# SiLU as one ScalarE function in the state space branch, and its norm one output unit later

## The chip, the cores and the metric

The kernel runs on one core of a Trainium2 chip. The metric is the device time of one execution in microseconds. TensorE (PE) multiplies matrices into PSUM banks, VectorE (DVE) does elementwise work, ScalarE (ACT) evaluates a function of scale times input plus bias, GpSimd (POOL) does a little elementwise work here, and the queue of SyncE (SP) issues the DMAs. Each engine works through its own instructions in order, and semaphores join the engines.

## The reference, cut to what matters

Two layers on a residual stream x of 512 tokens and 1024 channels. Each layer projects x into three branches, a state space branch (SSD), differential attention and cross-attention to 256 memory tokens; the branches are gated, summed, projected and normalised. The SSD branch is what the change touches:

```
xbc = silu(centred_dwconv(xbc, conv_w) + conv_b)         # 5 taps per channel, 3072 channels
xs, B, C = split(xbc)                                    # 2048, 4 x 128, 4 x 128 channels
dt = softplus(dt_raw + dt_bias); a = -exp(a_log)
y  = ssd_scan(xs*dt, dt*a, B, C) + the same backwards + d_skip*xs
y  = y * silu(z)
y_ssd = y * rsqrt(mean(y*y) + 1e-5) * norm_w             # mean over all 2048 channels
```

with silu(v) = v / (1 + exp(-v)) = v/2 * (1 + tanh(v/2)).

## The kernel before

Channels lie on the 128 partitions and the 512 tokens in the free dimension. All large products run in fp32r with each factor split in two (`split`: a rounded copy on ACT, the remainder on DVE) and three matmuls per pair. Weights come in units of 128x1024 values: one DMA into `wr` (2 buffers), the split into `wh` and `wl` (3 buffers each), then 24 matmuls of 512 columns into a bank `pj` (3 banks). `emit` walks a list of jobs (`self.T`), and asks for the weights of the next two units ahead of each job. The order of the jobs in the list is their priority; a planner at build time orders the instructions of every engine by priority and by when its own costs say that operands and buffers are there. `self.late` shifts priorities (`LX` for the transposes of xs, `LD` for the last product of a head pair).

The SSD branch of a layer runs over four groups g. A group has one unit for B, one for C, four for xs, then the chunk states, and then for b = 0 to 3 a unit for z (`zpart`) and the scan's output `ypart(g, b)` for two heads. Ready units of the next group fill PE while a `ypart` waits. From group 1 on the output units of the group before (`wpart(g-1, u)`) are listed behind the xs units; those of the last group stand at the end.

`conv` (from L432) brings one unit through convolution and SiLU. With `hcw`, half of the weights and bias, ACT writes `acc` from the PSUM bank with the centre tap, DVE adds four taps (`acc<-pj,hcw,acc`), ACT takes `th` = tanh(acc), and DVE forms (th + 1) * acc, which is the SiLU of twice `acc`. The result goes to `bC`, `cC` or `xsC` and from there to PE. `zpart` does the same on z, but without the half: `sz` = (tanh(z/2) + 1) * z is twice the SiLU, y is twice its value, and the epsilon of the norm is four times the reference's to make up for it.

`ypart` has per head a DMA that spreads a row of decays over all partitions (`ab<-dab`, 2 buffers), a mask on DVE (`ab<-ab,cst`), 8 `Exp` activations (`ab<-ab,bias`), and two DVE operations to `m`, which PE multiplies with `xsT` (`pm<-m,xsT`). Then DVE combines y, and ACT and DVE split it into `yh` and `yl`; ACT squares it into the buffer of `sz` (2 buffers), and POOL adds the square to `sqa`. `dt_tables`, once a layer in group 0, prepares the decays with `Exp`, `Ln` and `Exp` again.

`norm` multiplies the four blocks of `sqa` with ones on PE, takes a reciprocal root by 12 small DVE operations behind the mean, spreads it by matmuls with the identity, and ACT copies it to `rB`. `fin(j)` multiplies the gate and `rB` into the output rows. The end of the branch is listed as: gate units 0 and 1, `norm`, gate unit 2, `wpart(3, 0..3)`, and then gate units 3 to 7 with `fin(0..7)`. The gates take the tags `th` and `sz` with two buffers each.

Of the kernel before, what the change touches and what calls it, by code (L numbers as in the profile page):

```python
# [14 lines left out]
AF = mybir.ActivationFunctionType  # L15
ALU = mybir.AluOpType
# [4 lines left out]
P = 128  # L21
S = 512
# [4 lines left out]
EPS = 1e-5  # L27
# [6 lines left out]
PCW, PCB, PNW, PGB, PDN, PLG, PLB, PDS, NP_ = 0, 120, 144, 160, 184, 185, 193, 201, 217  # L34
# [17 lines left out]
def bc(ap, shape):  # L52
    return ap.broadcast_to(shape)


class Net:
# [243 lines left out]
    def layer_params(self, l):  # L300
        nc, a = self.nc, self.a
        pr = self.t(self.cp, [P, NP_], "pr", bufs=2)
        nc.sync.dma_start(out=pr, in_=a["pk"][l])
        self.par = pr
        self.hgb = self.t(self.cp, [P, 24], "hgb", bufs=2)
        self.ts(self.hgb, pr[:, PGB:PGB + 24], 0.5, ALU.mult)
        self.hcw = self.t(self.cp, [P, 144], "hcw", bufs=2)
        self.ts(self.hcw, pr[:, PCW:PCW + 144], 0.5, ALU.mult)


    def mem_kv(self, l):
# [121 lines left out]
    def conv(self, ps, ci, out):  # L433

        sp = self.sp
        acc = self.t(sp, [P, S], "acc", bufs=2)
        th = self.t(sp, [P, S], "th", bufs=2)
        cw = lambda j: self.hcw[:, ci * 5 + j:ci * 5 + j + 1]
        self.act(acc, ps, AF.Identity, scale=cw(2), bias=self.hcw[:, 120 + ci:121 + ci])
        for j in (-2, -1, 1, 2):  # L440
            o, i = slice(max(0, -j), S - max(0, j)), slice(max(0, j), S - max(0, -j))
            self.stt(acc[:, o], ps[:, i], cw(2 + j), acc[:, o], ALU.mult, ALU.add)
        self.act(th, acc, AF.Tanh)
        self.stt(out, th, 1.0, acc, ALU.add, ALU.mult)

    def ssd(self, l):
        nc = self.nc
# [75 lines left out]
        def zpart(g, b):  # L523
            def f(wh, wl):
                ps = self.proj(wh, wl)
                th = self.t(self.sp, [P, S], "th", bufs=2)
                self.act(th, ps, AF.Tanh, scale=0.5)
                self.sz = self.t(self.sp, [P, S], "sz", bufs=2)
                self.stt(self.sz, th, 1.0, ps, ALU.add, ALU.mult)
            return f  # L530

        def ypart(g, b):
# [56 lines left out]
        def wpart(g, u):  # L589
            def f(wh, wl):  # L590
                yh, yl = self.yhl[g]
                for i in range(2):
                    ps = self.bank(self.pj, "pj")
                    for k in range(4):
                        c = slice(k * 256 + i * P, k * 256 + (i + 1) * P)
                        self.mm3(ps, wh[:, c], wl[:, c], yh[:, k, :], yl[:, k, :], k == 0, k == 3)
                    o = self.br[:, 2 * u + i, :]
                    if g == 0:
                        self.act(o, ps)
                    else:  # L600
                        self.tt(o, o, ps, ALU.add)
            return f
# [6 lines left out]
        def norm():  # L609
            sp = self.sp  # L610

            pt = self.bank(self.pt, "pt")
            for c in range(4):
                self.mm(pt[:, c:c + 1], self.sqa[:, c * P:(c + 1) * P], self.ones[:, 0:1])
            ms = self.t(sp, [P, 4], "ms")
            self.ts(ms, pt[:, 0:4], 1.0 / 2048.0, ALU.mult, 4.0 * EPS, ALU.add)
            r = self.rsqrt(sp, ms, 4)
            pr = self.bank(self.pm, "pm")
            for c in range(4):
                self.mm(pr[:, c * P:(c + 1) * P], bc(r[:, c:c + 1], [P, P]), self.ident)  # L620
            self.rB = self.t(sp, [P, S], "acc", bufs=2)
            self.act(self.rB, pr)

        def gpart(j):
            def f(wh, wl):
                self.gt[j] = self.gate(self.sp, wh, wl, 0, j, "th" if j % 4 < 2 else "sz")
            return f

        def fin(j):
            def f():  # L630
                t, o = self.gt.pop(j), self.br[:, j, :]
                self.stt(t, t, 1.0, self.rB, ALU.add, ALU.mult)
                self.tt(o, o, t, ALU.mult)
            return f
# [29 lines left out]
        self.gt = {}  # L664
        for j in range(3):
            self.T(gpart(j), (l, UGL + j))
            if j == 1:
                self.T(norm)
        for u in range(4):
            self.T(wpart(3, u), (l, UBS + 12 + u))  # L670
        for j in range(KC):
            if j + 3 < KC:
                self.T(gpart(j + 3), (l, UGL + j + 3))
            self.T(fin(j))
# [638 lines left out]
```

## Time and profile before

| | |
|---|---|
| time, median of 3 runs | 2211.78 us (2208.17 to 2215.52) |
| the profiled execution | 2208.37 us, of which the span of the instructions is 2206.5 us |
| granted TensorE clock, mean | 0.995 |
| PE, DVE, ACT busy | 2158.8, 1609.6, 1022.9 us |
| the SSD branch in the trace, layer 0 and layer 1 | about 20 to 460 us, and 1150 to 1615 us |
| ACT table loads | 7, 9.0 us |

The profile shows one execution. Busy shares of PE are not its distance from full speed: matmuls overlap. What PE could still gain is read from what it waits for. "A <- B: us, times" in a list of waits says that A stood idle until B ended. In a row of the chain or of a time line the first number is the start in microseconds from the first instruction, the second the duration; the time in square brackets is the engine's idle time before it. Names are written as output<-inputs, and L103 is line 103.

### The profile page before, as it was taken

To read this page: it belongs to the slowest core of one execution; us is meant where nothing else is said; L and a number is where in the kernel's file an instruction comes from. 1 tells how busy PE (TensorE), PEld (TensorE's weight loads), DVE (VectorE), ACT (ScalarE), POOL (GpSimd) and SP (SyncE) were. 2 spreads that over 40 slices of the span, in tenths; PEclk is the share of its full clock that TensorE was granted. 3 is DMA by queue.
4 is the path that set the end of the run, shared out by engine and by line. 5 is a ranking of instruction groups with operands and counts; after the bars stand their busy time and mean duration, and the time that the engine had idled before them with its cause. 6 is when DMAs were issued, how large, how long until landed. Compare 5 with 4: busy or idle time off the path is not lost.

```text
span 2206.5 us, 29202 instructions
## 1 busy us (share of the span) xinstructions
PE 2158.8 (98%) x11122; PEld 1780.2 (81%) x11122; DVE 1609.6 (73%) x2486; ACT 1022.9 (46%) x1935; POOL 52.7 (2%) x38
## 2 busy tenths in 40 slices
PE   8999999999999999999999999999999999999998
PEld 6777877778888888887887777777788888888876
DVE  7897888858554778866467887888754547788667
ACT  5664546424432555543345564555423325555430
POOL 0000000000000000000000000000100000000000
PEclk9999999999999999999999999999999999999999
DMA  4654544335553433324564654444434334333253
GB/s 151 172 171 129 157 133 147 111 95 174 164 170 120 134 110 111 108 88 153 157 220 111 169 143 143 143 141 137 120 99 130 111 109 136 111 110 106 90 159 109
DMA packets 109680, 295.27 MB, mean 134 GB/s; under 512 B 12460, under 2 KB 13028, under 8 KB 109284
## 3 DMA queue, kind: packets, MB, share of 16 engines
q1 hardware_dynamic: 109540, 293.41, 44.1%
q8 instruction: 87, 1.43, 0.3%
q14 instruction: 53, 0.43, 0.1%
HBM read 255.06 MB, written 17.33 MB: 123 GB/s over the span
## 4 chain that ended last, share of the span: by engine, by line
PE 76%; DVE 11%; DMA 7%; ACT 3%; issue 2%; POOL 0%; SPq 0%; POOLq 0%; DVEq 0%; ACTq 0%
PE pj L103 59%; PE pm L103 15%; DMA ab<-dab 5%; PE pt L111 2%; DVE ab L81 2%; DVE wl L81 2%; DVE acc L84 2%; DVE y L81 1%; DMA wr<-wu 1%; ACT wh L91 1%; ACT ab L91 1%; DVE yl L84 1%; DVE m L81 1%; DMA fth<-rd 1%; DVE eb L81 1%
## 5 line engine op out<-in xcount | busy, mean ns | idle before, releaser
L103 PE MATMUL pj<-xh,wl 128*128 128x512 f32 x1664 | 663.8, 399 | 5.5 <-ACT mrg L91 3.8
L103 PE MATMUL pj<-xh,wh 128*128 128x512 f32 x1664 | 659.5, 397 | 6.9 <-ACT xh L91 6.0
L103 PE MATMUL pj<-xl,wh 128*128 128x512 f32 x1664 | 658.7, 396 | 0.0
L81 DVE TENSOR_TENSOR wl<-wr,wh 128x1024 fp32r<-128x1024 f32 x330 | 404.8, 1227 | 102.4 <-ACT wh L91 101.9
L91 ACT ACTIVATE wh<-wr 128x1024 fp32r<-128x1024 f32 x330 | 347.3, 1053 | 215.8 <-PE pj L103 139.5
L103 PEld LDWEIGHTS pj<-xh,wh 128*128 128x128 f32 x1664 | 313.5, 188 | 79.1 <-ACT xh L91 6.0
L103 PEld LDWEIGHTS pj<-xh,wl 128*128 128x128 f32 x1664 | 313.6, 188 | 76.5 <-ACT mrg L91 5.5
L103 PEld LDWEIGHTS pj<-xl,wh 128*128 128x128 f32 x1664 | 313.8, 189 | 66.2 <-issue 4.2
L91 ACT ACTIVATE ab<-ab,bias 128x128 f32<-128x128 f32 x512 | 160.7, 391 | 117.9 <-DVE ab L81 116.1
L84 DVE SCALAR_TENSOR_TENSOR acc<-pj,hcw,acc 128x510 f32<-128x510 f32 (+1 forms) x192 | 141.6, 742 | 26.5 <-ACT acc L91 25.5
L941 DVE TENSOR_REDUCE fmx<-pm 128x1 f32<-128x512 f32 x128 | 85.0, 685 | 47.0 <-PE pm L103 47.0
L103 PE MATMUL pj<-yl,wh 128*128 128x512 f32 x256 | 103.8, 406 | 0.8 <-DVE yl L84 0.8
L103 PE MATMUL pj<-yh,wh 128*128 128x512 f32 x256 | 104.4, 408 | 0.0
L103 PE MATMUL pj<-dy,wh 128*128 128x512 f32 (+1 forms) x384 | 102.6, 356 | 1.3 <-DVE dy L81 1.3
L81 DVE TENSOR_TENSOR ab<-ab,cst 128x1024 f32<-128x1024 f32 x64 | 85.7, 1338 | 24.1 <-DMA ab<-dab 24.0
L103 PE MATMUL pj<-yh,wl 128*128 128x512 f32 x256 | 103.2, 404 | 0.1
L91 ACT ACTIVATE fpp<-pm,fmx 128x512 f32<-128x512 f32 x128 | 87.2, 686 | 33.6 <-DVE fmx L941 33.6
L103 PE MATMUL pj<-cy,wh 128*128 128x512 f32 x256 | 78.8, 389 | 0.0
L103 PEld LDWEIGHTS pj<-dy,wh 128*128 128x128 f32 x384 | 67.5, 188 | 13.7 <-DVE dy L81 2.6
L103 PE MATMUL pj<-wh,xl 128*128 128x256 f32 x256 | 73.3, 286 | 0.0
L103 PE MATMUL pj<-wl,xh 128*128 128x256 f32 x256 | 72.4, 283 | 0.0
L103 PE MATMUL pj<-wh,xh 128*128 128x256 f32 x256 | 72.4, 283 | 0.0
(280 smaller groups left out, 3317.2 us busy)
## 6 DMA issues: line engine op xcount, KB each, us to landing
wr<-wu SPq DMA_DIRECT2D x336, 512.0 KB, 3.7
ab<-dab SPq DMA_DIRECT2D x64, 512.0 KB, 5.6
eb<-deb SPq DMA_DIRECT2D x64, 256.0 KB, 4.8
mkv<-dkv SPq DMA_DIRECT2D x16, 512.0 KB, 3.9
rsw<-rx SPq DMA_DIRECT2D x64, 128.0 KB, 2.3
dy<-dy SPq DMA_DIRECT2D x32, 256.0 KB, 2.3
dgt<-tg SPq DMA_DIRECT2D x16, 256.0 KB, 4.2
dkv<-mo SPq DMA_DIRECT2D x16, 256.0 KB, 4.3
```

What stands on the lines that cost most here:

```text
L81: (eng or self.nc.vector).tensor_tensor(out=out, in0=a, in1=b, op=op)
L84: self.nc.vector.scalar_tensor_tensor(out=out, in0=a, scalar=s, in1=b, op0=op0, op1=op1)
L91: self.nc.scalar.activation(out=out, in_=a, func=f, **kw)
L103: self.nc.tensor.matmul(out=out, lhsT=a, rhs=b, start=first, stop=last)
L111: self.nc.tensor.transpose(out=out, in_=x, identity=self.ident)
L941: nc.vector.tensor_reduce(out=mx[:, c:c + 1], in_=ps, axis=AX.X, op=ALU.min)
```

## The change

In `conv` the full weights and bias are used in place of their halves, `hcw` is gone, and ACT's own SiLU function writes the result from `acc`; the tile `th` and the DVE operation behind it are gone. In `zpart` ACT's SiLU writes `sz` straight from the PSUM bank; again `th` and one DVE operation are gone. As y is no longer doubled, the norm's epsilon is the reference's. `norm` moves in the list from behind gate unit 1 to behind `wpart(3, 0)`, past gate unit 2 and that output unit.

```
@@ layer_params
-        self.hcw = self.t(self.cp, [P, 144], "hcw", bufs=2)
-        self.ts(self.hcw, pr[:, PCW:PCW + 144], 0.5, ALU.mult)
@@ conv
-        th = self.t(sp, [P, S], "th", bufs=2)
-        cw = lambda j: self.hcw[:, ci * 5 + j:ci * 5 + j + 1]
-        self.act(acc, ps, AF.Identity, scale=cw(2), bias=self.hcw[:, 120 + ci:121 + ci])
+        cw = lambda j: self.par[:, PCW + ci * 5 + j:PCW + ci * 5 + j + 1]
+        self.act(acc, ps, AF.Identity, scale=cw(2), bias=self.par[:, PCB + ci:PCB + ci + 1])
...
-        self.act(th, acc, AF.Tanh)
-        self.stt(out, th, 1.0, acc, ALU.add, ALU.mult)
+        self.act(out, acc, AF.Silu)
@@ zpart
-                th = self.t(self.sp, [P, S], "th", bufs=2)
-                self.act(th, ps, AF.Tanh, scale=0.5)
                 self.sz = self.t(self.sp, [P, S], "sz", bufs=2)
-                self.stt(self.sz, th, 1.0, ps, ALU.add, ALU.mult)
+                self.act(self.sz, ps, AF.Silu)
@@ norm
-            self.ts(ms, pt[:, 0:4], 1.0 / 2048.0, ALU.mult, 4.0 * EPS, ALU.add)
+            self.ts(ms, pt[:, 0:4], 1.0 / 2048.0, ALU.mult, EPS, ALU.add)
@@ the list of the branch's end
         for j in range(3):
             self.T(gpart(j), (l, UGL + j))
-            if j == 1:
-                self.T(norm)
         for u in range(4):
             self.T(wpart(3, u), (l, UBS + 12 + u))
+            if u == 0:
+                self.T(norm)
```

## The prediction

> **What bounds the kernel now.** I read the page's busy times and its chain first, then the list of what PE waits for, then the busy times in the two stretches in which the state space branch (SSD) runs.
>
> ```profile
> PE 2158.8 (98%) x11122; PEld 1780.2 (81%) x11122; DVE 1609.6 (73%) x2486; ACT 1022.9 (46%) x1935; POOL 52.7 (2%) x38
> ...
> PE 76%; DVE 11%; DMA 7%; ACT 3%; issue 2%; POOL 0%; SPq 0%; POOLq 0%; DVEq 0%; ACTq 0%
> ```
>
> PE carries 76% of the chain and is hardly ever idle. Work taken from DVE, or put on ACT, counts only where PE stops for it. PE's waits over the whole span say how much there is to win; these are the rows whose tiles belong to the SSD branch (us in total, times, longest).
>
> ```profile
> PE pm L103 <- DVE m L81: 8.3, 8, 2.2
> ...
> PE pt L103 <- POOL sqa L81: 4.4, 2, 2.4
> PE pm L103 <- DVE xw L81: 4.4, 2, 2.6
> PE pj L103 <- ACT mrg L91: 3.8, 4, 2.3
> ...
> PE pt L111 <- DVE bC L84: 1.0, 2, 0.7
> ...
> PE pm L103 <- DVE cC L84: 0.8, 2, 0.5
> ```
>
> Together they are 22.7 us, 1.0% of the time. The change takes nothing from PE itself, so this is about the ceiling of a gain; a loss has no such ceiling. The room on the other engines is in the table of stretches (length, then PE, PEld, DVE, ACT, POOL busy us; layer 0, then layer 1):
>
> ```profile
> 60.00:455.00 395.00, 385.30 (x1943) 303.51 (x1942) 332.54 (x456) 211.59 (x450) 26.46 (x16) 1.00 0.49 145
> 1190.00:1607.00 417.00, 403.05 (x2017) 317.90 (x2016) 343.63 (x475) 217.06 (x458) 24.98 (x16) 0.99 0.50 141
> ```
>
> DVE is at 84% and 82%, ACT at 54% and 52%. So the change takes load from the fuller of the two.
>
> **The SiLU: what goes.** Groups by line and shape, of ACT and of DVE:
>
> ```profile
> L91 ACT ACTIVATE th<-acc 128x512 f32<-128x512 f32 x48 | 30.2, 629 | 39.3 <-DVE acc L84 39.3
> ...
> L91 ACT ACT_TABLE_LOAD x7 | 9.0, 1283 | 0.8 <-PEq L1304 0.7
> ```
> ```profile
> L84 DVE SCALAR_TENSOR_TENSOR xsC<-th,acc 128x512 f32<-128x512 f32 x32 | 22.0, 687 | 4.0 <-ACT th L91 4.0
> L84 DVE SCALAR_TENSOR_TENSOR sz<-th,pj 128x512 f32<-128x512 f32 x32 | 21.9, 685 | 27.5 <-ACT th L91 23.6 <-POOL sqa L81 3.6
> ```
>
> The 48 convolutions and the 32 z units each lose one DVE operation, 80 x 0.686 = 54.9 us of DVE. The profile has no SiLU activation. The nearest row is the tanh of the same shape, 629 ns, and I take the same: ACT's pure work stays. The scaling of the convolution's weights once a layer, at the layer's head, I cost at nothing either way; PE is then busy with the products before it.
>
> What does it win on the path? The waits for `bC` and `cC` (1.0 + 0.8) are each shorter than the 0.69 us that leave their chain, so they go: **-1.8 us** (from 0 to -1.8). For the 8 waits on `m` I looked into the chain of waits, in group 0 of both layers:
>
> ```profile
> 99.15 0.60 DVE sz L84
> 99.75 0.61 DVE ab L81
> ...
> 100.38 0.70 DVE m L81
> ```
> ```profile
> 1239.98 0.60 DVE sz L84
> ...
> 1252.39 0.60 DVE sz L84
> ```
>
> Three times the removed operation stands in DVE's queue right ahead of the sum and the product that make `m`. 3 x 0.60 gives **-1.8 us**. The bounds are 0, if DVE's queue only closes up behind the mask's DMA, and -8.3, if all of these waits go.
>
> **The SiLU: what comes.** Seven table loads in the whole kernel show that tanh and `Exp` share a table (they alternate without one), and that other functions do not share it. Around `Ln` in `dt_tables`:
>
> ```profile
> 52.64 1.28 ACT L91 ACT_TABLE_LOAD   x1
> 54.91 0.42 ACT L91 ACTIVATE bias<-bias 128x256 f32<-128x256 f32 x1 [0.99 <-DVE bias L88]
> ```
> ```profile
> 58.12 0.28 ACT L91 ACTIVATE cum<-pm 128x128 f32<-128x128 f32 x1 [1.00 <-PE pm L103]
> 58.42 1.28 ACT L91 ACT_TABLE_LOAD   x1
> 59.71 0.63 ACT L91 ACTIVATE th<-acc 128x512 f32<-128x512 f32 x1
> 60.25 0.26 ACT L91 ACTIVATE dtot<-pm 128x128 f32<-128x128 f32 x1
> 60.41 1.06 ACT L91 ACTIVATE eb<-pt 64x512 f32<-64x512 f32 x2
> ```
>
> Whether SiLU stands in `Exp`'s table no row can say; the nearest rows, of `Ln` and back, say no, and I take that. Counting in ACT's order every change between a future SiLU (`th<-acc`, and `th` of z) and an `Exp` (`dtot`, `wst`, `ab<-ab,bias`), as from the row at 59.71 to the row at 60.25, I get 102 changes. That is 102 x 1.283 = 131 us more on ACT, 65 us in each stretch, which brings it to 70% and 68%. The bounds of the number of loads are 0 and, if the planner mixes more, about 160 (two for each of 80 SiLUs).
>
> How much of a load delays anybody? The first pair of rows shows the mechanism: the load runs at once, while the function behind it still waits for its operand, and costs nothing. The second shows the other case: ACT is late, and `th` starts 1.31 us after `cum` ends. `Exp` mostly waits:
>
> ```profile
> ACT ab L91 <- DVE ab L81: 116.1, 37, 5.5
> ```
>
> 37 waits of 3.1 us on average cover 37 of the 51 loads ahead of an `Exp`; 14 of 51, 27%, stay open. Ahead of a convolution's SiLU the wait is 39.3 us in all (row of `th<-acc`), 0.8 for each of 48; I count half of these loads as open. So about (14 + 25) x 1.28 = 50 us of lateness lies on ACT in stretches where it has 383 us idle. Weights do not suffer: in PE's waits above, ACT appears for `mrg` alone.
>
> On the path this gives three terms. (1) `dt_tables`, once a layer: in the rows above `dtot` and `eb` (an `Exp` each) come right behind a `th` with no pause, and the rows that PE waits for (`xw`, twice) hang on them. One more load each: **+2.6 us** (from 0 to two loads each, +5.1). (2) The 8 waits on `m` lengthen by the open 27% of a load: 8 x 0.27 x 1.28 = **+2.8 us**. (3) The four waits on `mrg`, by the mean open share 39 of 102: 4 x 0.38 x 1.28 = **+2.0 us**. The bounds of (2) and (3) are 0 and what the rivals below make of them.
>
> One wait changes engine. The DVE row of `sz` has waited 3.6 us for POOL, which still reads the old square out of the buffer. Now ACT writes `sz` itself and would stand there, with the next weight split and the next head's `Exp`s queued behind it. I put it at zero, as the planner holds the SiLU back until it sees the buffer free.
>
> The Trainium skill (ScalarE: Activation LUTs, section What ACT_TABLE_LOAD costs) speaks against this change: it counts a drain of about 1380 ns beside the 1283 ns, 2.66 us for each change of set. By that the 102 changes would be an estimated 271 us. The trace disagrees: from the end of `cum` at 58.40 to the start of `th` at 59.71 there is room for the load and nothing else.
>
> **The norm.** In the chain at the end of layer 0's branch (a unit of 24 matmuls is the measure):
>
> ```profile
> 422.64 5.49 PE pj L103 x24
> ...
> 449.25 1.27 POOL sqa L81
> ...
> 450.56 1.05 PE pt L103 x8
> ```
>
> PE stands until POOL has added the last square. Moved past a gate unit and an output unit, the sums come up to 11 us later in PE's list, while POOL is 2.4 us late at most: the wait goes, **-4.4 us** for both layers (0, if the planner had already placed the output unit ahead). What moves: 8 matmuls on `sqa`, 13 small DVE operations, 8 spreading matmuls, one ACT copy; no DMA. Behind it stand the `fin`s, which need `rB`; three further output units, 3 x 5.49 = 16.5 us, cover that. What would be late next is `wpart(3, 0)` itself, which needs the last `yl`; it needs it only for the last quarter of its first bank, 9 matmuls in, 9 x 5.49/24 = 2.1 us, and the gate unit ahead of it gives 5.5 us more. If that cover is gone, the part of POOL's lateness that DVE shares returns, at most the 4.4 us.
>
> **The sum**, against the profiled execution: -1.8 - 1.8 + 2.6 + 2.8 + 2.0 - 4.4 = -0.6 us on 2208.4, so 2207.8. The median of the runs lies 3.4 us above that execution; I predict for the median, 2211.8 - 0.6 = **2211 us**. A difference within 0.3% (6.6 us) is what a measurement can't tell from none.
>
> **Rivals.** *DVE's relief carries further.* The waits on `m`, `bC`, `cC` and `sqa` all vanish: -14.5 + 2.6 = -11.9, 2200 us. For it: DVE at 84%, the chain through `sz`. Against it: those heads also wait for the mask's DMA. *No loads*, SiLU shares the table: -1.8 - 1.8 - 4.4 = -8.0, 2204 us. Against it: the loads around `Ln`. *The switch lands on the heads without slack.* In the first heads of a layer and the last, PE waits for `m` with nothing else to do (8 times). If the z SiLU falls between such a head's mask and its `Exp`s, or waits for POOL there, the head gets a load to SiLU and one back, 2.57 us: 8 x 2.57 = 20.5, and 5.1 in `dt_tables`, less 4.4 and 1.8: +19.4, 2231 us. It decides as soon as four of the eight are hit (4 x 2.57 + 5.1 - 6.2 = +9.2). *ACT's order becomes the bound.* No load is covered, and each of the 32 `ypart`s is late by one: 32 x 1.28 - 6.2 = +34.8, 2247 us. Against it: the 37 waits of `Exp`. The skill's 2.66 us would make it likelier; the gap of 1.31 us keeps it small.
>
> **How the numbers follow.** My forecast 0.42; further relief 0.25; no loads 0.05; heads without slack 0.20; ACT as the bound 0.08. So faster 0.30, same 0.42, slower 0.28. The range runs from all 22.7 us of waits gone (2189) to just over the heads without slack (2234); it leaves out the last rival. The forecast's own range is 2205 to 2218.
>
> **What would show it.** About 100 table loads of 1.28 us, most with an idle ACT behind them; a row of SiLU at 0.6 us; DVE down by 55 us; PE's wait for `sqa` gone and none for `yl` over 1 us; PE's wait for `xw` up to near 3.5 us each. Wrong is the forecast if the waits on `m` move by more than 6 us either way, or if PE starts to wait for `wh` or `wl` in the SSD stretches.

## The result, and the profile after

The changed kernel takes 2220.91 us (median of 6 runs, 2219.69 to 2224.9), the kernel before, timed beside it, 2209.98 (2203.42 to 2215.52): a ratio of 1.0054, 95% interval 1.0037 to 1.0070. It is slower, by about 11 us. The profiled execution took 2220.79 us against 2208.37.

The page of the changed kernel, busy times and chain:

```profile
PE 2160.7 (97%) x11122; PEld 1781.9 (80%) x11122; DVE 1563.5 (70%) x2404; ACT 1169.9 (53%) x2047; POOL 46.7 (2%) x38
...
PE 73%; DVE 11%; DMA 9%; ACT 4%; issue 2%; SPq 0%; DVEq 0%; ACTq 0%
```

DVE has lost 82 operations and 46 us, ACT has gained 147 us. ACT's groups by shape say what it gained:

```profile
L91 ACT ACT_TABLE_LOAD x119 | 152.7, 1283 | 48.3 <-DVE acc L84 24.7 <-PE pj L103 14.4 <-DVE ab L81 6.3
...
L91 ACT ACTIVATE xsC<-acc 128x512 f32<-128x512 f32 x32 | 20.2, 633 | 15.8 <-DVE acc L84 15.5
...
L91 ACT ACTIVATE sz<-pj 128x512 f32<-128x512 f32 x32 | 19.1, 598 | 25.3 <-PE pj L103 24.8
```

SiLU costs what tanh did (0.63 and 0.60 us), and there are 112 more table loads. The two stretches of the SSD branch (length, then PE, PEld, DVE, ACT, POOL, granted clock):

```profile
60.00:455.00 395.00, 379.50 (x1900) 299.30 (x1899) 305.02 (x404) 277.36 (x498) 21.14 (x15) 0.99 0.49 143
1190.00:1607.00 417.00, 399.51 (x1982) 315.68 (x1981) 323.37 (x436) 289.90 (x513) 21.72 (x15) 0.98 0.48 138
```

ACT is at 70% in both, DVE at 77% and 78%. Neither is full, and yet PE does less in the same time. What PE waits for (us in total, times, longest):

```profile
PE pt L111 <- ACT bC L91: 18.5, 5, 5.8
...
PE pm L103 <- DVE xw L81: 5.2, 4, 1.7
PE pj L103 <- DVE mrg L81: 4.0, 4, 1.3
PE pj L103 <- DVE wl L81: 3.6, 4, 2.3
PE pm L103 <- DVE m L81: 2.7, 4, 1.2
PE pj L103 <- DVE acc L84: 2.2, 2, 1.1
...
PE pj L103 <- DVE yl L84: 0.6, 2, 0.3
PE pj L103 <- ACT mrg L91: 0.5, 2, 0.2
```

Most old waits shrank: `m` from 8.3 to 2.7, those for `sqa` and `cC` are gone. One grew out of nearly nothing: **`bC`, from 1.0 to 18.5 us**, in five stops of up to 5.8 us. `bC` is B after its convolution, the first thing of a new group that PE needs beside the projections. There are six such seams between groups, three in each layer; 17.9 of the 18.5 us lie at four of them, those into groups 2 and 3.

One seam, from group 1 to group 2 of layer 0. VectorE's time line before (the four `acc` rows from 228.82 to 233.13 are the taps of B):

```profile
218.41 0.69 DVE L81 TENSOR_TENSOR m<-ab,gs 128x512 f32<-128x512 f32 x1
...
222.35 1.22 DVE L81 TENSOR_TENSOR ab<-ab,cst 128x1024 f32<-128x1024 f32 x1
...
225.97 2.33 DVE L81 TENSOR_TENSOR ab<-ab,cst 128x1024 f32<-128x1024 f32 x1
...
228.82 0.73 DVE L84 SCALAR_TENSOR_TENSOR acc<-pj,hcw,acc 128x510 f32<-128x510 f32 x1
...
233.13 0.73 DVE L84 SCALAR_TENSOR_TENSOR acc<-pj,hcw,acc 128x510 f32<-128x510 f32 x1
```

and after:

```profile
219.72 1.22 DVE L81 TENSOR_TENSOR ab<-ab,cst 128x1024 f32<-128x1024 f32 x1 [3.59 <-DMA ab<-dab]
220.86 0.68 DVE L81 TENSOR_TENSOR ab<-ab 128x512 f32<-128x512 f32 x1
...
223.99 0.68 DVE L81 TENSOR_TENSOR m<-ab,gs 128x512 f32<-128x512 f32 x1
...
229.60 0.74 DVE L84 SCALAR_TENSOR_TENSOR acc<-pj,pr,acc 128x510 f32<-128x510 f32 x1
...
232.05 1.21 DVE L81 TENSOR_TENSOR ab<-ab,cst 128x1024 f32<-128x1024 f32 x1
233.18 0.74 DVE L84 SCALAR_TENSOR_TENSOR acc<-pj,pr,acc 128x511 f32<-128x511 f32 x1
234.91 1.23 DVE L81 TENSOR_TENSOR ab<-ab,cst 128x1024 f32<-128x1024 f32 x1 [0.98 <-DMA ab<-dab]
...
236.71 0.74 DVE L84 SCALAR_TENSOR_TENSOR acc<-pj,pr,acc 128x510 f32<-128x510 f32 x1
```

B's convolution starts 0.8 us later and ends 3.6 us later: two masks now stand **between its taps**, and one of them waits for the DMA that brings the row to be masked. Counted in order, with eight heads to a group, they are the masks of the first two heads of group 2. Before, the first of the two stood ahead of the taps, at 225.97, and the second long behind them, at 249.96. The second's DMA is not later now (issued at 228.61, before at 230.22); the new order has brought its mask forward by 15 us, to a place where the row has not landed. The first mask is late because its DMA is, and that DMA waits for a buffer that the last `ypart` of group 1 still holds. ScalarE's time line of that `ypart` in the changed kernel:

```profile
214.76 2.44 ACT L91 ACTIVATE ab<-ab,bias 128x128 f32<-128x128 f32 x8
...
218.26 1.28 ACT L91 ACT_TABLE_LOAD   x1 [1.06 <-PE pj L103]
219.56 0.60 ACT L91 ACTIVATE sz<-pj 128x512 f32<-128x512 f32 x1
221.01 1.28 ACT L91 ACT_TABLE_LOAD   x1 [0.85 <-DVE ab L81]
222.30 2.45 ACT L91 ACTIVATE ab<-ab,bias 128x128 f32<-128x128 f32 x8
```

The z SiLU and its two loads stand ahead of the second head's eight `Exp`s. Those of the first head (214.76) are over at 217.2, ahead of the loads and no later than before. What holds the first head up is VectorE's order. Before, its `m` (218.41) came ahead of the second head's mask (222.35). Now that mask (219.72) comes ahead of the sum (`ab<-ab`, 220.86) that the first head's `m` needs, and VectorE, which works in order, stands 3.59 us for the mask's DMA. So the first head's `m` starts at 223.99, 5.6 us later than before, and only then is its `ab` buffer free for the first row of group 2. The DMA queue issues that row's DMA 6.3 us later than before; before:

```profile
219.17 0.37 SPq L558 DMA_DIRECT2D ab<-dab  x1
```

after:

```profile
225.44 3.56 SPq L552 DMA_DIRECT2D ab<-dab  x2
```

and PE stops at the transposes of `bC`, which started at 236.38 before:

```profile
240.40 0.66 PE L111 MATMUL pt<-cst,bC 128*128 128x128 f32 x4 [3.42 <-ACT bC L91]
```

Of these 4.0 us the taps make 3.6. The rest lies behind the last tap, where four `Exp`s, B's own load and the SiLU now stand in place of tanh and the product. The picture is the same at all four seams with a long stop: VectorE stands 3.6 to 4.2 us at the second head's mask, where before it took up the first head's `m` first. At the two seams into group 1 VectorE has no such stand and PE does not stop, though one mask stands between B's taps there too.

Over the whole kernel the mask's wait for its DMA went from 24.0 us (the first row, before) to 50.0 (the second, after):

```profile
L81 DVE TENSOR_TENSOR ab<-ab,cst 128x1024 f32<-128x1024 f32 x64 | 85.7, 1338 | 24.1 <-DMA ab<-dab 24.0
```
```profile
L81 DVE TENSOR_TENSOR ab<-ab,cst 128x1024 f32<-128x1024 f32 x64 | 79.0, 1234 | 50.0 <-DMA ab<-dab 50.0
```

The stops add up. Two rows of PE's waits before that the prediction didn't count:

```profile
PE pj L103 <- DVE wl L81: 2.5, 2, 1.7
...
PE pj L103 <- DVE yl L84: 0.8, 4, 0.2
```

The SSD rows of the prediction made 22.7 us, with `yl` 23.5; the rows above without `wl` make 33.7, and `wl` adds 1.1: +11.3 of the 12.4 us between the two profiled executions.

### The profile page after: what moved, and what is told of

The parts are those of the page before. It is cut to its first block, busy times and chain, and to the rows that moved or that the text cites. A ratio compares the mean times of both kernels' runs of the same rounds, so it can differ in the third digit from the quotient of the medians.

```text
span 2219.0 us, 29227 instructions
## 1 busy us (share of the span) xinstructions
PE 2160.7 (97%) x11122; PEld 1781.9 (80%) x11122; DVE 1563.5 (70%) x2404; ACT 1169.9 (53%) x2047; POOL 46.7 (2%) x38
## 4 chain that ended last, share of the span: by engine, by line
PE 73%; DVE 11%; DMA 9%; ACT 4%; issue 2%; SPq 0%; DVEq 0%; ACTq 0%
PE pj L103 56%; PE pm L103 14%; DMA ab<-dab 5%; DMA wr<-wu 2%; PE pt L111 2%; DVE wl L81 2%; DVE acc L84 2%; DVE ab L81 1%; DVE y L81 1%; DVE m L81 1%; DMA fth<-rd 1%; ACT wh L91 1%; ACT ab L91 1%; ACT L91 1%; DVE eb L81 1%
## 5 line engine op out<-in xcount | busy, mean ns | idle before, releaser
L91 ACT ACT_TABLE_LOAD x119 | 152.7, 1283 | 48.3 <-DVE acc L84 24.7
L84 DVE SCALAR_TENSOR_TENSOR acc<-pj,pr,acc 128x510 f32<-128x510 f32 (+1 forms) x192 | 142.3, 744 | 25.5 <-ACT acc L91 24.1
L81 DVE TENSOR_TENSOR ab<-ab,cst 128x1024 f32<-128x1024 f32 x64 | 79.0, 1234 | 50.0 <-DMA ab<-dab 50.0
L91 ACT ACTIVATE fpp<-pm,fmx 128x512 f32<-128x512 f32 x128 | 87.2, 685 | 33.7 <-DVE fmx L935 33.6
```

The costliest lines, as they stand in the source:

```text
L81: (eng or self.nc.vector).tensor_tensor(out=out, in0=a, in1=b, op=op)
L84: self.nc.vector.scalar_tensor_tensor(out=out, in0=a, scalar=s, in1=b, op0=op0, op1=op1)
L91: self.nc.scalar.activation(out=out, in_=a, func=f, **kw)
```

## The experiments

All were timed in rounds with the kernel before, whose median lay between 2209.4 and 2210.5. Medians and intervals of all runs stand in the table behind the last experiment. "Masks" there is counted in VectorE's time line: the masks that stand between the first and the fourth tap of B at the six seams (24 taps).

### The two parts alone

The kernel before with only the norm moved:

```
-            if j == 1:
-                self.T(norm)
...
+            if u == 0:
+                self.T(norm)
```

> The kernel before with the norm alone moved behind the last group's first output unit; SiLU stays tanh, sum and product. All theories: TensorE's wait for the squares' sum (4.4 us, two times) goes, the rest stays: ratio 0.996 to 1.000 against the kernel before, about 2206 us. If the moved norm is what costs the change its 11 us, it is 2215 us or more.

Measured 2203.48 us, ratio 0.9971 (0.9962 to 0.9981): 6.0 us faster, and faster than both kernels. The other part alone, the change with the norm at its old place (the same lines the other way round):

> The changed kernel with the norm at its old place, so the SiLU alone. If the two parts add up, it loses the 6 us that the moved norm alone was worth: 2224 to 2230 us, and TensorE's wait for the squares' sum is back with about 4 us. If the moved norm wins nothing beside the SiLU, 2219 to 2222 us.

2227.41 us. It is 6.5 us over the whole change, so the norm's gain is the same in both surroundings, and the SiLU costs 17.4 us.

### Loads, or the order that the planner makes for them

The planner counts a table load in its costs, so the change does two things: it brings loads, and it makes the planner order every engine anew. Three kernels separate these. First the change with tanh in place of SiLU in both places (SiLU is left out), which needs 7 loads as before:

```
-        self.act(out, acc, AF.Silu)
+        self.act(out, acc, AF.Tanh)
...
-                self.act(self.sz, ps, AF.Silu)
+                self.act(self.sz, ps, AF.Tanh)
```

> The changed kernel with tanh in place of ScalarE's SiLU in both places; this leaves the SiLU out of the result, and keeps every operation and its size, without the table loads, in the order that the planner makes when it sees no loads. Theory L (the loads cost): 2196 to 2206 us, below the kernel before, since the waits of the last product and the norm shrink and the wait for bC is gone. Theory S (writing bC, cC and sz straight from ScalarE costs, loads or not, because ScalarE's queue is in order): 2215 us or more, with TensorE's wait for bC still over 10 us.

2207.10 us. Then the order of that kernel with SiLU put back into the finished program, so that the loads come upon an order that knows nothing of them:

```
+    for f in nc.python_module().functions:
+        for b in f.blocks:
+            b.instructions = [copy.replace(i, func=AF.Silu) if i.name in names else i for i in b.instructions]
```

> The changed kernel's SiLU in the instruction order of the kernel with tanh in its place: the planner saw no loads, the chip has about 98 new ones. It computes the whole reference. Theory Q (the loads delay ScalarE's queue by themselves): 2215 to 2230 us, near the changed kernel or over it. Theory P (the planner, which charges the loads, makes a worse order, with Exps ahead of bC): 2200 to 2210 us.

2256.46 us: **+49 us for 96 loads**, beyond both expectations. And the other way, the changed kernel's own order with SiLU exchanged for tanh in the finished program (SiLU is left out), so that 112 loads drop out:

> The changed kernel, instruction for instruction in its own order on every engine, with tanh in place of SiLU at the end, so that 114 table loads fall out and nothing else changes; this leaves the SiLU out of the result. Theory Q (loads delay the queue): 2203 to 2212 us, TensorE's wait for bC below 6 us. Theory P (the order is what costs): 2216 to 2221 us, the wait for bC still over 12 us.

2214.86 us, between the two expectations. From the norm alone the steps are +3.6 (one pass, no loads), +7.8 (the order made for the loads) and +6.0 (the loads in that order); by the intervals each step is uncertain by 3 to 4 us. So about half of the loads' price is the order itself, and in the order made without them they cost eight times the 6 us.

The profile of this last kernel (an execution of 2208.4 us) has the ten masks between the taps and VectorE's stand at the four seams, 3.4 to 3.7 us, without the loads. So the loads are not needed to make the rows late in this order. They add at the end: PE waits 9.7 us for `bC` in place of 18.5, and 7.0 us of the difference is shorter time from the last tap to B's function.

### Which half

SiLU in one pass for the convolution alone, z as before, and for z alone, the convolution as before; both with the norm moved. The edits are the two halves of the diff (with tanh's z, the epsilon stays 4 * EPS).

> The changed kernel with SiLU in one pass for the convolution alone; z goes by tanh, sum and product again (75 table loads in place of 119). Theory D (every load costs about the same, (2220.9 - 2207.1) / 112 = 0.12 us of the time): near 2214 us. Theory B (the loss lies at the groups' seams, where TensorE waits for bC): nearly the whole loss stays, 2216 to 2222 us, with TensorE's wait for bC over 12 us.

> The kernel with the moved norm and SiLU in one pass for z alone; the convolution goes by tanh, sum and product (58 table loads). Theory D: 2203.5 + 51 x 0.12 and a part of the 3.6 us that the one pass costs without loads, near 2211 us. Theory B: no loss at the seams, 2202 to 2207 us, and no wait for bC over 3 us.

2206.38 and 2225.53 us. Against the norm alone, the convolution with 68 more loads costs 2.9 us, z with 51 more loads costs 22.0. Every reading in which a load has one price falls. None of the three kernels of this section came out where either theory expected it. The reading that the stop at `bC` comes from `bC`'s own SiLU alone falls as well; in the z-only kernel DVE writes `bC` as before, and PE stops all the same:

```profile
PE pt L111 <- DVE bC L84: 14.3, 5, 4.5
```

The same with B and C alone by tanh, xs and z by SiLU:

```
+        if two:
+            self.act(th, acc, AF.Tanh)
+            self.stt(out, th, 1.0, acc, ALU.add, ALU.mult)
+        else:
+            self.act(out, acc, AF.Silu)
```

> The changed kernel with B and C alone by tanh, sum and product (with half weights as before); xs and z keep ScalarE's SiLU (97 table loads). Theory B: the wait for bC is below 4 us and the time 2203 to 2211 us. Theory D: 2207.1 + 90 x 0.12, 2216 to 2220 us.

2227.29 us, with 15.6 us of stops at `bC`. The symptom is at the seam; its cause lies in the z half.

### The z half: direct write, order or loads

z in one pass with tanh (z's SiLU is left out), planned without loads:

> The norm moved, the convolution as before, z in one pass that writes sz straight from the bank, but with tanh instead of SiLU, so 7 table loads (z's SiLU is left out: sz is tanh(z)); the planner counts without loads. If the 22 us of the z half come from the loads and from the order that makes room for them: 2203-2208, PE's wait for bC under 4 us. Rival W (they come from the direct write: ACT stands for POOL, which still reads the old square out of the buffer of sz): 2216-2226, with PE's wait for bC over 8 us.

2196.56 us, 6.9 us *below* the norm alone and below what either theory expected: that ACT writes `sz` itself costs nothing. Whether DVE's relief or the new order gives the 6.9 us is not separated; the tanh kernel, with the relief of both halves, lies 3.6 us above the norm alone. The z-only kernel's own order, with the SiLU exchanged for tanh in the finished program (left out again):

> The z-only kernel (median 2225.5) in its own order on every engine, with the SiLU replaced by tanh after planning, so that its 51 extra loads drop out (z's SiLU is left out). If the order that the planner chose for these loads is what costs: 2216-2226. If the loads themselves do: 2203-2209. By the split of the whole change (7.8 us order to 6.0 us loads) in between: 2211-2217, and PE's wait for bC falls from 14.3 to about 8 us.

2223.69 us. PE's waits in the first and in the second of these:

```profile
PE pt L111 <- DVE bC L84: 1.9, 3, 0.7
```
```profile
PE pt L111 <- DVE bC L84: 14.4, 4, 4.3
```

Of the 29 us between z by tanh and z by SiLU, **27.1 are the order and 1.8 the loads**, and the 1.8 are within the noise. In the second of these kernels VectorE stands 3.7 to 4.1 us at the second head's mask at the four seams, with no load more than before; in the first 0.8 to 1.6 us. My expectation of a split like that of the whole change was wrong.

### A third buffer for the decay rows

If the order is bad because a late `m` holds an `ab` buffer, a third one takes the reason away. Its room comes from the gates, whose tag `th` moves to the buffers of `m`:

```
-                    ab = self.t(sp, [P, 2, 4, P], "ab", bufs=2)
+                    ab = self.t(sp, [P, 2, 4, P], "ab", bufs=3)
...
-                self.gt[j] = self.gate(self.sp, wh, wl, 0, j, "th" if j % 4 < 2 else "sz")
+                self.gt[j] = self.gate(self.sp, wh, wl, 0, j, *(("m", 3) if j % 4 < 2 else ("sz", 2)))
```

> The changed kernel with a third buffer for the decay rows (ab), for which the gates' tag th gives its room (they use the buffers of m). Everything is computed. Theory Z (the z unit's SiLU and its two table loads make a head's m late, so the ab buffer comes free late, so the next group's first decay rows land late, and their mask and Exps stand ahead of B's convolution in DVE's and ACT's queues): the DMA no longer waits for m, PE's wait for bC falls from 18.5 us to under 8, and the time to 2208-2214. Rival T (bC is late because ACT itself is late by its loads, whatever the buffers do): the wait stays at 14 to 20 us and the time at 2218-2224.

The control has the second edit alone:

> The control of the kernel with three ab buffers: the changed kernel with two, but the gates' tag th moved to the buffers of m in the same way. Theory Z and rival T both expect the changed kernel's time, 2218-2224, with PE's wait for bC at 15 to 21 us; a difference from it is the price of the gates' buffers and is to be taken off.

With three buffers 2197.19 us, ratio 0.9939 (0.9925 to 0.9952); the control 2223.07. So 26 us, more than I expected (2208 to 2214 us): the changed kernel turns from 11 us slower than before into 13 us faster. PE's wait for `bC`, the mask's wait for its DMA, and VectorE at the same seam:

```profile
PE pt L111 <- ACT bC L91: 0.7, 1, 0.7
```
```profile
L81 DVE TENSOR_TENSOR ab<-ab,cst 128x1024 f32<-128x1024 f32 x64 | 78.3, 1226 | 15.7 <-DMA ab<-dab 15.3
```
```profile
211.16 1.22 DVE L81 TENSOR_TENSOR ab<-ab,cst 128x1024 f32<-128x1024 f32 x1
...
216.28 0.68 DVE L81 TENSOR_TENSOR ab<-ab 128x512 f32<-128x512 f32 x1
...
226.66 1.22 DVE L81 TENSOR_TENSOR ab<-ab,cst 128x1024 f32<-128x1024 f32 x1
227.79 0.74 DVE L84 SCALAR_TENSOR_TENSOR acc<-pj,pr,acc 128x510 f32<-128x510 f32 x1
...
230.03 0.74 DVE L84 SCALAR_TENSOR_TENSOR acc<-pj,pr,acc 128x511 f32<-128x511 f32 x1
...
231.29 2.17 DVE L84 SCALAR_TENSOR_TENSOR acc<-pj,pr,acc 128x511 f32<-128x511 f32 x3
```

The second head's mask (211.16) still stands ahead of the first head's sum (216.28), but its row is there, at this seam and at the other three. The last mask stands ahead of the taps again, and no DMA is waited for. The whole order is a new one as well, so what the buffer does in an order that stays was not tried.

### Is it the buffer, whatever the SiLU does?

Two kernels without the extra loads get the third buffer: the tanh kernel (SiLU left out), and the kernel before with the norm moved. The second finds the room by halving the weights in place and by giving `tg` the buffers of `m`; its control has that and two buffers.

```
-        self.hcw = self.t(self.cp, [P, 144], "hcw", bufs=2)
-        self.ts(self.hcw, pr[:, PCW:PCW + 144], 0.5, ALU.mult)
+        self.hcw = pr[:, PCW:PCW + 144]
+        self.ts(self.hcw, self.hcw, 0.5, ALU.mult)
...
-                    self.gate_ahead(l, i, j, lambda: self.sp, "tg")
+                    self.gate_ahead(l, i, j, lambda: self.sp, "m")
```

> The changed kernel with tanh in place of SiLU in both places (SiLU is left out, 7 table loads) and with the third ab buffer; with two it took 2207.1. If the buffers bound the branch in every version (theory G): 2193-2199, a gain of 8 to 14. If the third buffer only repairs what the loads and their order do (theory L): 2203-2209, and the changed kernel's 2197 is by then better than any version without loads.

> The kernel before with the norm moved (2203.5) and a third ab buffer; the room comes from halving the convolution's weights in place and from tg, which uses the buffers of m. Everything is computed, 7 loads. Theory G: 2190-2197, the best of all; PE's waits for m (6.1 us) and for bC stay small. Theory L: within 3 us of its control.

> Control of the last: the kernel before with the norm moved, the weights halved in place and tg in the buffers of m, but two ab buffers. Both theories: 2200-2208, as with the norm alone (2203.5); what it differs from that is the price of making room.

2204.69, 2211.81 and 2209.99 us: 2.4 us less than the tanh kernel with two buffers (which has no control for the moved tag), 1.8 more than the control. Making the room costs the second 6.5 us by itself. In the orders that the planner makes without loads, the third buffer gives next to nothing; both have four masks between the taps. Then the loads themselves, with the buffer there (the order of the three-buffer kernel, SiLU exchanged for tanh in the finished program, SiLU left out):

> The changed kernel with three ab buffers (2197.2) in its own order on every engine, the SiLU replaced by tanh after planning, so that its 92 extra loads drop out (SiLU is left out). With two buffers the loads cost 6.0 us in the same test. If the third buffer covers them: 2194-2198, under 3 us. If they cost what they did: 2190-2192.

2197.38 us against 2197.19 with its 92 extra loads. In this order they cost **nothing that can be measured**. This kernel has the same instructions as the tanh kernel with three buffers (2204.69): the order that was made for the loads is 7.3 us better than the one that was made without them. So what a third buffer is worth where there are no loads stays open.

### Does it repeat?

Two more slow kernels get the third buffer, with edits as above: the one with the norm at its old place, and z alone.

> The SiLU in one pass with the norm at its old place (2227.4 with two ab buffers) and a third ab buffer, room from the gates as before. Everything is computed. If the buffer takes away the change's own loss: 2200-2208, PE's wait for bC (20.1 us) under 4 us; the norm's 6 us stay lost. If the order was luck: anything from 2200 to 2230, most likely over 2212.

> The z-only SiLU with the norm moved (2225.5 with two ab buffers) and a third one, room from the halving in place and from tg, which cost the kernel without loads 6.5 us. Everything is computed. If the buffer takes away the change's own loss: 2198-2210, PE's wait for bC (14.3 us) under 4 us. If the order was luck: over 2214.

2196.42 us, 31 below the same with two buffers; and 2217.28, only 8 below, against my 2198 to 2210. The first differs from the earlier kernel with three buffers (2197.19) in the norm's place alone, so it is not an independent repeat. It also shows that the norm's move, worth 6 us with two buffers, is worth nothing with three; I had expected those 6 us to stay lost. The second makes its room as the norm kernel did, and has no control for that. In it no mask stands between the taps any more, but PE still stops:

```profile
PE pt L111 <- DVE bC L84: 15.7, 6, 3.3
PE pm L103 <- DVE m L81: 15.1, 7, 6.8
```

VectorE's time line shows another place, ahead of the last `ypart` of the group:

```profile
228.25 1.23 DVE L81 TENSOR_TENSOR ab<-ab,cst 128x1024 f32<-128x1024 f32 x1 [4.11 <-DMA ab<-dab]
```

This is the mask of the next group's first head. DVE's queue stands 4.1 us for its row (4.0 to 4.3 us at the four seams), and the convolution, behind it, starts late as a whole. The order is again one in which an early mask waits; why the planner put it there was not followed up.

| kernel | loads | median us | ratio to before (95%) | wait for `bC` us | masks |
|---|---|---|---|---|---|
| before | 7 | 2209.98 | | 1.0 | 0 |
| changed | 119 | 2220.91 | 1.0054 (1.0037 to 1.0070) | 18.5 | 10 |
| norm alone | 7 | 2203.48 | 0.9971 (0.9962 to 0.9981) | 1.3 | 0 |
| SiLU alone | 119 | 2227.41 | 1.0076 (1.0060 to 1.0092) | 20.1 | 10 |
| tanh in its place | 7 | 2207.10 | 0.9988 (0.9976 to 1.0000) | 3.8 | 0 |
| that order, SiLU | 103 | 2256.46 | 1.0221 (1.0206 to 1.0236) | 23.1 | 0 |
| changed order, tanh | 7 | 2214.86 | 1.0022 (1.0012 to 1.0032) | 9.7 | 10 |
| convolution only | 75 | 2206.38 | 0.9985 (0.9974 to 0.9996) | 1.0 | 0 |
| z only | 58 | 2225.53 | 1.0055 (1.0033 to 1.0077) | 14.3 | 8 |
| B, C by tanh | 97 | 2227.29 | 1.0076 (1.0060 to 1.0091) | 15.6 | 9 |
| z only, tanh | 7 | 2196.56 | 0.9941 (0.9929 to 0.9953) | 1.9 | 1 |
| z-only order, tanh | 7 | 2223.69 | 1.0059 (1.0045 to 1.0072) | 14.4 | 8 |
| gates' tag moved | 119 | 2223.07 | 1.0052 (1.0039 to 1.0064) | 16.2 | 10 |
| that and 3 buffers | 99 | 2197.19 | 0.9939 (0.9925 to 0.9952) | 0.7 | 0 |
| that order, tanh | 7 | 2197.38 | 0.9944 (0.9929 to 0.9959) | 0 | 0 |
| tanh, 3 buffers | 7 | 2204.69 | 0.9976 (0.9964 to 0.9989) | 11.6 | 4 |
| norm, room | 7 | 2209.99 | 0.9995 (0.9983 to 1.0008) | 1.3 | 0 |
| norm, room, 3 buffers | 7 | 2211.81 | 1.0010 (1.0000 to 1.0020) | 7.4 | 4 |
| SiLU alone, 3 buffers | 99 | 2196.42 | 0.9939 (0.9921 to 0.9957) | 0.7 | 0 |
| z only, room, 3 buffers | 58 | 2217.28 | 1.0038 (1.0023 to 1.0053) | 15.7 | 0 |

The waits and masks are those of one profiled execution, which can lie some us from the median (2214.9 us for "tanh in its place", 2208.4 for "changed order, tanh").

With two buffers, the kernels whose order has 8 to 10 masks between the taps take 2215 to 2227 us, and those with 0 or 1 2197 to 2210, except for the order that was blind to its loads. That is a close companion of the loss, not proof that the masks alone carry it: the last row has none and is slow, and two of the changed kernel's ten stand where PE does not stop.

## Why the prediction was wrong

Forecast: 2211 us with the old and the new terms in balance, 42% for no change. Measured: 2220.9, slower, inside the range and above the forecast's own 2205 to 2218. Step by step:

**Sizes on the engines: right.** 112 more loads where I counted 102, 1.283 us each; SiLU at 0.60 to 0.63 us; ACT at 70% in both stretches where I had 70% and 68%. DVE fell by 46 us, not 55.

**The norm, -4.4 us: right,** 6.0 measured alone with two buffers, and nothing with three. The wait for `sqa` is gone, `yl` waits 0.6 us and none for over 1 us.

**What goes (-1.8 for `bC` and `cC`, -1.8 for `m`): half.** `cC` went; `m` fell by 5.6 us, with my +2.8 for the loads not to be seen. What DVE's relief is worth on the path, no run separates from the new orders.

**ACT writing `sz`, at nothing: right,** by z in one pass with tanh (2196.56 us).

**What comes: the step that failed.** The sentence is "On the path this gives three terms". `dt_tables` (+2.6) came out as +0.8 on the waits for `xw`, `mrg` (+2.0) as +0.7 (0.5 + 4.0 less 3.8). The term that decided was not among them: +17.5 at `bC`. I looked for the loads' lateness only where PE waited already, and I took the order of every queue as given. Neither holds. The planner counts the loads and orders all engines anew. In the new order VectorE takes up a second head's mask ahead of the first head's sum and stands 3.6 to 4.2 us for its DMA; `m`, the `ab` buffer and the next group's first DMA come late, and that group's masks stand between B's taps. In the rival at 2231 us I had loads hit a head's `Exp`s, and priced that at the eight waits on `m`. The rows show the first head held up by VectorE's order and not by the loads, and the price is paid at `bC`.

**The cover of the loads, ahead of these terms: wrong as well.** From the row at 52.64 I took it that a load runs while its function still waits, and let 73% of the loads ahead of an `Exp` go free. In the changed kernel no load but the first is followed by more than 0.02 us of idle ACT. Ahead of 32 of them ACT stands idle (46.1 of the 48.3 us in their row), as at 218.26 and 221.01: the load starts when the wait is over, and the function comes the load's 1.28 us later. So the sign "most with an idle ACT behind them" failed too. My 50 us of open lateness on ACT was near the 49 us that the loads cost in an order that is blind to them, and far from the 6.0 and 0 us that they cost in orders that count them. As those 50 us are time on ACT and not on the path, this nearness is luck.

The Trainium skill (ScalarE: Activation LUTs, section What ACT_TABLE_LOAD costs) counts a drain of about 1380 ns beside each load's 1283. The changed kernel's rows agree with the 1283 and not with the drain: after the load at 221.01 the `Exp`s start at 222.30, 1.29 us later.

Shown by runs: the loss lies in the z half, where all but 1.8 of 29 us are order; in the whole change it is 7.8 us of order and 6.0 of loads; and the third buffer, with the order that comes with it, removes the loss in two nearly equal kernels and not in the z-only one. Argued from the time lines: the chain from VectorE's stand at the second head's mask over `m` and the `ab` buffer to the taps of B; no run changes that place alone. Open: why the planner picks such an order, and the z-only kernel with three buffers.

## What to carry to other kernels

When a tool orders the instructions, an edit is also a new order: split its price by exchanging the function in the finished order, in both directions, before blaming the operation. Kernels of the same instructions in two orders differed here by 7 to 36 us. Then look in the in-order queues for an operation that stands for a DMA ahead of work whose operands are there. One more buffer for that DMA, with the order that came with it, here turned +11 us into -13 us. Counting loads, or the waits that exist already, finds neither.

## What the hardware showed that I had not expected

The price of a table load on the path ranged from nothing (92 loads, -0.2 us) over 0.05 us (112 loads, 6.0) to 0.5 us (96 loads, 49.4), always with the same 1.28 us on ACT and with ACT idle for about a third of the stretch. Here are the stretches of the order that was blind to its loads, and of the kernel with three buffers:

```profile
60.00:455.00 395.00, 370.80 (x1813) 290.32 (x1813) 296.33 (x385) 252.72 (x463) 19.34 (x13) 0.97 0.49 138
1190.00:1607.00 417.00, 389.85 (x1891) 303.39 (x1889) 311.74 (x415) 265.92 (x478) 17.12 (x12) 0.98 0.46 130
```
```profile
60.00:455.00 395.00, 387.43 (x1958) 305.96 (x1957) 310.38 (x412) 266.92 (x492) 27.95 (x16) 1.00 0.49 145
1190.00:1607.00 417.00, 406.32 (x2051) 321.10 (x2050) 324.86 (x445) 276.38 (x504) 31.23 (x16) 1.00 0.49 142
```

The slowest order has the lower ACT load (64% of each stretch against 68% and 66%), as it gets less done in the same time (463 operations of ACT in the first stretch against 492). In these profiles the granted TensorE clock goes with the stops: 0.97 and 0.98 in the slowest kernel, 0.99 and 0.98 in the changed one, 1.00 in that with three buffers. PE's busy time for the same 11122 matmuls is 2160.7 us in the changed kernel and 2153.4 with three buffers:

```profile
PE 2153.4 (98%) x11122; PEld 1776.5 (81%) x11122; DVE 1558.7 (71%) x2404; ACT 1142.9 (52%) x2027; POOL 60.4 (3%) x38
```

So 7 of the 21 us between their two spans (2219.0 and 2198.0) lie in PE's busy time. In the changed kernel's trace the granted clock is 0.50 from 351.5 to 358.2, 1389.1 to 1395.8 and 1505.2 to 1511.9 us, stretches that begin in three of the four seam stops; at the fourth it is 1.00 (236 to 246). With three buffers it is 1.00 in the first and the last of these stretches. That the stops lower it fits, but no run tried it by itself.
